# A hybrid decoder layer on one core: the first branch's projection in seven products of quarters, the scores by head pairs

## The chip, the cores and the metric

One core of one Trainium2 chip runs the whole layer. The metric is the device time of one execution in microseconds; the time before is the median of three runs.

## The reference

The layer takes `x` of 256 tokens by 2048 channels. One input projection feeds two token mixers and two gates; each mixer's output is widened by a gate, projected to 2048 channels, merged, projected once more, normed and added to `x`. Everything is float32. Cut to what matters:

```python
h = rms_norm(x, pre_norm_w)
proj = h @ w_in                          # 2048 x 12304
gdn_qkv, gdn_z, gdn_b, gdn_a, moba_qkv, moba_z, gate_a, gate_b = split(proj)
qkv = silu(causal_depthwise_conv(gdn_qkv, conv_w))        # 4 taps
qa, ka, va = ...                         # 8 heads of 128, q and k l2-normed
beta, g = sigmoid(gdn_b), -exp(a_log) * softplus(gdn_a + dt_bias)
oa = gated_delta_rule(qa, ka, va, beta, g)   # chunks of 64: a triangular inverse each
oa = rms_norm_per_head(oa) * gdn_norm_w * silu(gdn_z)
u_a = oa @ w_branch_a                    # 1024 x 2048
ob = causal_softmax_attention(qb, kb, vb)    # 8 heads of 128; one block of 256 here
ob = ob * silu(moba_z)
u_b = ob @ w_branch_b                    # 1024 x 2048
merged = sigmoid(gate_a) * u_a + sigmoid(gate_b) * u_b
y = merged @ w_out                       # 2048 x 2048
out = x + rms_norm(y, post_norm_w)
```

## The kernel before

Tokens lie in two tiles of 128 (`t`), channels in 16 row blocks of 128. A float32 product is made of three reduced-precision ones: each operand is split into `hi` (ScalarE, a cast) and `lo` (VectorE, value minus `hi`), and TensorE adds hi·hi, hi·lo and lo·hi. Weights come through SyncE's queue in pieces of 1 MB (`raw`, three buffers) and are split by `split` (L211) in halves of 128x1024 elements, with three buffers for `hi` and three for `lo`.

Two forms of projection are used. `proj_n` (L347) gives tokens by 512 channels: 12 matmuls of 128x512 for each half. `proj_t` (L329) gives two heads transposed: 8 pairs of a 128x512 and a 128x256 matmul for each half. A `product` (L986) is one quarter (512x512) of the output projection, 12 matmuls for each token tile.

The order of the projections is written out by hand in `ORDER`: names are queries and keys of the first mixer (`q`, `kq`), its values (`v`), its gate (`zg`), the second mixer's values, gate and heads (`mv`, `zm`, `mk`; `mk` makes an `mq` and an `mk` projection for two heads) and the two merge gates (`ga`, `gb`, four column blocks each). The smaller work is written as generators in `Queue`s. After every 6 matmuls of `proj_n` and `product`, and every 8 of `proj_t`, `tick` (L132) counts each queue's wait down by 0.5; when it is up, the next step is issued there, in the midst of a projection. The values yielded are those waits: `SC_WAIT` before a head's scores, `LC_WAIT`, `INV` and `L_WAIT` round the triangular inverse, `SV_WAIT` and `OS_WAIT` in the solve, `A_WAIT1` to `4` in attention.

- `scores` (L491), one head at a time: a split of key and query (`kq`), scores, decays.
- `inverse` (L598): the chunks go to DRAM and back regrouped (`l_d`, `lc`), VectorE makes the inverse in 63 steps (`tv`, `tw`), which goes to DRAM and back (`t_d`, `tt`) by the GpSimd queue.
- `solve` (L695): small matmuls (`sv`, `so`), the norm and gate (`oz`), then `turned_outputs` (L773) transposes by token tile and splits into `oaT`.
- `attend` (L812): scores `ms`, softmax `s`, transposes `pp`, values `po`, the gated output `om`, and its transpose `pt` into `obT`.
- After all gates, a loop over the four column blocks makes `ua` (48 matmuls), multiplies it into `ga`, makes `ub` (48 matmuls), multiplies it into `gb`, and queues `merge` (L925): the sum, transposes `mt`, the split into `mT`, and sums of quarters (`sums`, `sf`).
- The output projection does the upper half of its rows for the first two column blocks in seven quarter products (`yp1` to `yp7`) instead of eight, by sums of quarters of `mT` and differences of quarters of the weights (`tq`, fetched by the GpSimd queue). Third-block pieces `third` (`y2`) lie between. Four PSUM banks (c11, c12, c21, c22) gather the results; `s1`, `s5` and `v` keep copies.

```python
def differences():                       # L917
    yield 3
    for o, a, b in ((0, 0, 2), (1, 1, 0), (2, 1, 2)):
        for u in range(2):
            us = slice(2 * u, 2 * u + 2)
            nc.vector.tensor_tensor(tq[o][:, us], tq[a][:, us], tq[b][:, us], op=ALU.subtract)
            yield 1
```

Each engine runs its instructions in the order in which they were issued; a tile shares its place with another of the same tag, and waits until that one's readers are done.

Of the kernel before, what the change touches and what calls it, by code (L numbers as in the profile page):

```python
# [15 lines left out]
P = 128  # L16
# [10 lines left out]
L_WAIT = 7  # L27
LC_WAIT = (2, 2, 2, 4)
INV = (0.6, 2)
SLOW = 8  # L30
V_WAIT = 8
SV_WAIT = 1
OS_WAIT = 5
# [39 lines left out]
def hybrid_layer(  # L73
# [52 lines left out]
    aq = [Queue(), Queue()]  # L126
# [4 lines left out]

    def tick():  # L132
        after[0] -= 0.5
        for q in (gq, vq, mq, *aq, *extra):
            q.tick()
# [177 lines left out]
    for t in range(NT):  # L313
        dg = wk.tile([P, P], F32, tag="f256", bufs=6, name=f"dg_{t}")
        nc.vector.tensor_scalar_mul(dg, ident, rstd[:, t : t + 1])
        mm(prr[:, t * P : (t + 1) * P], ones, dg, start=True, stop=True)
# [131 lines left out]
    def halves(pt, name):  # L448
        y = wk.tile([P, S], F32, tag="f256", bufs=6, name=f"y_{name}")
# [41 lines left out]
    def scores(h, kT, qT):  # L491
        kq = big.tile([P, 2, 2 * S], F32R, tag=("tt", "tw")[h % 2], name=f"kq_{h}")
        for i, y in enumerate((kT, qT)):
            nc.scalar.copy(kq[:, i, :S], y)
            nc.vector.tensor_tensor(kq[:, i, S:], y, kq[:, i, :S].bitcast(F32), op=ALU.subtract)
        yield SC_WAIT
        p1 = aux_tile(f"s1_{h}")
# [83 lines left out]
    def queries(p):  # L581
        h = 2 * p
        pq = proj_t(CQ + h * P, f"q{h}")
        qTs = [halves(pq[m], f"q{h + m}") for m in range(2)]
        for m in range(2):
            conv_silu(qTs[m], h + m)
        for m in range(2):
            gq.add(scores(h + m, kTs[p][m], qTs[m]))
        if p == H // 2 - 1:
            gq.add(inverse())  # L590
            gq.add(solve())
# [86 lines left out]
    ga = big.tile([P, D // 512, NT, 512], F32, tag="ga", name="ga")  # L678
# [6 lines left out]
    ob_tile = lazily(lambda: free_tile([P, H, 2 * S], F32R, "g0", "obT"))  # L685

    def sigmoid_gate(n, col, c):
        pts = proj_n(w_in, col + c * 512, hT, KT, f"{n}{c}")
        for t in range(NT):
            tl = ga if n == "ga" else gb_tile()  # L690
            nc.scalar.activation(tl[:, c, t, :], pts[t], AF.Sigmoid, scale=rstd[:, t : t + 1])

    oaT = [None]

    def solve():  # L695
# [77 lines left out]
        def turned_outputs(t, oz):  # L773
            for g in range(2):
                pt = aux_tile(f"ot_{t}_{g}")
                for hh in range(4):
                    tr(pt[:, hh * P : (hh + 1) * P], oz[:, g, hh, :], ident)
                p3 = pt.rearrange("p (h n) -> p h n", n=P)
                hi = oT[:, g * 4 : g * 4 + 4, t * P : (t + 1) * P]
                lo = oT[:, g * 4 : g * 4 + 4, S + t * P : S + (t + 1) * P]  # L780
                gn = pcol[:, NTAP * NCV : NTAP * NCV + 1]
                nc.scalar.activation(hi, p3, AF.Copy, scale=gn)
                nc.vector.scalar_tensor_tensor(
                    lo, p3, gn, hi.bitcast(F32), op0=ALU.mult, op1=ALU.subtract
                )
                yield 0.5

# [10 lines left out]
        for t in range(NT):  # L798
            yield from normed(t, ozs[t])
        yield OS_WAIT  # L800
        for t in range(NT):
            yield from turned_outputs(t, ozs[t])
# [9 lines left out]
    def attend(h, qT, kT):  # L812
# [26 lines left out]
        om = wk.tile([P, NT, P], F32, tag="om", name=f"om_{h}")  # L839
        for t in range(NT):  # L840
            nc.vector.scalar_tensor_tensor(
                om[:, t, :], po[:, t * P : (t + 1) * P], sm[:, t : t + 1], zm()[:, t, hc], op0=ALU.mult, op1=ALU.mult
            )
        yield A_WAIT4
        pt = aux_tile(f"pt_{h}")
        for t in range(NT):
            tr(pt[:, t * P : (t + 1) * P], om[:, t, :], ident)
        obT = ob_tile()
        nc.scalar.copy(obT[:, h, :S], pt[:, :S])
        nc.vector.tensor_tensor(obT[:, h, S:], pt[:, :S], obT[:, h, :S].bitcast(F32), op=ALU.subtract)  # L850

    def attention(p):
# [7 lines left out]
        for m in range(2):  # L860
            aq[m].add(attend(h + m, qTs[m], kTs[m]))

# [7 lines left out]
    for blk in ORDER:  # L870
# [11 lines left out]
        elif n == "mk":  # L882
            attention(c)
        else:
            sigmoid_gate(n, {"ga": CGA, "gb": CGB}[n], c)


    gq.drain()
    for q in aq:
        q.drain()  # L890
    mT = big.tile([P, KT, 2 * S], F32R, tag="hT", name="mT")

# [10 lines left out]
    sf = big.tile([P, 4, 4, P], F32, tag="z0", name="sums_f")  # L903


    tq = [None, None, None]

    def load_quarter(i, h, c):
        tq[i] = big.tile([P, 4, 512], F32, tag=f"z{i}", name=f"tq_{i}")
        nc.gpsimd.dma_start(  # L910
            tq[i], wo[h * 512 : (h + 1) * 512, c * 512 : (c + 1) * 512].rearrange("(k p) c -> p k c", p=P)
        )

    load_quarter(1, 1, 1)
    load_quarter(2, 0, 0)

    def differences():  # L917
        yield 3
        for o, a, b in ((0, 0, 2), (1, 1, 0), (2, 1, 2)):
            for u in range(2):  # L920
                us = slice(2 * u, 2 * u + 2)
                nc.vector.tensor_tensor(tq[o][:, us], tq[a][:, us], tq[b][:, us], op=ALU.subtract)
                yield 1

    def merge(c, wait=1):  # L925
        yield wait
        for t in range(NT):
            nc.vector.tensor_tensor(ga[:, c, t, :], ga[:, c, t, :], gb_tile()[:, c, t, :], op=ALU.add)
        yield 0.5
        p3s = []  # L930
        for t in range(NT):
            pt = aux_tile(f"mt_{c}_{t}")
            for q in range(4):
                tr(pt[:, q * P : (q + 1) * P], ga[:, c, t, q * P : (q + 1) * P], ident)
# [9 lines left out]
        if c == 1:  # L944
# [9 lines left out]
            load_quarter(0, 0, 1)  # L954
            formed.append(True)
            sq.add(differences())

    formed = []
    sq = Queue()
    extra.append(sq)  # L960

    for c in range(D // 512):
        pa = proj_n(wa, c * 512, oaT[0], H, f"ua{c}")
        for t in range(NT):
            nc.vector.tensor_tensor(ga[:, c, t, :], ga[:, c, t, :], pa[t], op=ALU.mult)
        pb = proj_n(wb, c * 512, ob_tile(), H, f"ub{c}")
        for t in range(NT):
            nc.vector.tensor_tensor(gb_tile()[:, c, t, :], gb_tile()[:, c, t, :], pb[t], op=ALU.mult)
# [3 lines left out]
    sq.drain()  # L972
    while not formed:
        mq.tick()

    def quarter(t, h):

        ks = slice(4 * h, 4 * h + 4)
        return mT[:, ks, t * P : (t + 1) * P], mT[:, ks, S + t * P : S + (t + 1) * P]

    def load(h, c):
        raw = wraw.tile([P, 4, 512], F32, tag="raw", name=f"raw_y{c}_{h}")
        nc.sync.dma_start(raw, wo[h * 512 : (h + 1) * 512, c * 512 : (c + 1) * 512].rearrange("(k p) c -> p k c", p=P))
        return raw

    def product(a, raw, banks, first, name):  # L986

        for u in range(2):
            hi, lo = split(raw[:, 2 * u : 2 * u + 2, :], [P, 2, 512], f"{name}_{u}")
            for kk in range(2):  # L990
                k = 2 * u + kk
                for (ah, al), pt, new in zip(a, banks, first):
# [133 lines left out]
```

## Time and profile before

| | |
|---|---|
| runs, us | 781.89, 779.69, 779.84 (median 779.84) |
| the profiled execution, us | 780.75 |
| its span, us | 778.8 |
| mean granted TensorE clock | 0.996 |
| TensorE busy | 768.0 us, 99% of the span |
| VectorE busy | 530.7 us, 68% |
| ScalarE busy | 412.1 us, 53% |
| GpSimd busy | 24.6 us, 3% |
| read from and written to HBM | 145.42 and 3.15 MB |

PE is TensorE, DVE VectorE, ACT ScalarE, POOL GpSimd, SP SyncE. In the timeline a line has the start, the duration, the engine, the line of the code, the operation, output and inputs, their shapes, the number of instructions drawn together, and in brackets the idle time before with what ended it. In the groups the numbers after the count are busy time and mean ns of one, then idle time before. In the slices: busy time and count of PE, weight loads, DVE, ACT and POOL, the granted clock, the DMA share and GB/s. A DMA line ends with the KB of one and the median us from issue to landing.

### The profile page before, as it was taken

To read this page: it belongs to the slowest core of one execution; us is meant where nothing else is said; L and a number is where in the kernel's file an instruction comes from. 1 tells how busy PE (TensorE), PEld (TensorE's weight loads), DVE (VectorE), ACT (ScalarE), POOL (GpSimd) and SP (SyncE) were. 2 spreads that over 40 slices of the span, in tenths; PEclk is the share of its full clock that TensorE was granted. 3 is DMA by queue.
4 is the path that set the end of the run, shared out by engine and by line. 5 is a ranking of instruction groups with operands and counts; after the bars stand their busy time and mean duration, and the time that the engine had idled before them with its cause. 6 is when DMAs were issued, how large, how long until landed. Compare 5 with 4: busy or idle time off the path is not lost.

```text
span 778.8 us, 10308 instructions
## 1 busy us (share of the span) xinstructions
PE 768.0 (99%) x3947; PEld 655.4 (84%) x3947; DVE 530.7 (68%) x876; ACT 412.1 (53%) x623; POOL 24.6 (3%) x47
## 2 busy tenths in 40 slices
PE   8999999999999999999999999999999999999996
PEld 7898988898888888888888888888888888888884
DVE  5787668887864898976444665555644668986673
ACT  5677665655565545455435647354454445465451
POOL 3000000010020000001100000000000000000000
PEclk9999999999999999999999999999999999999999
DMA  8576675467479555656943455555456555577442
GB/s 304 169 226 221 185 217 163 134 196 210 162 214 280 180 203 178 201 187 205 230 135 109 152 174 168 187 162 186 162 185 228 183 197 203 192 271 270 166 158 109
DMA packets 92823, 149.24 MB, mean 192 GB/s; under 512 B 3045, under 2 KB 46694, under 8 KB 92134
## 3 DMA queue, kind: packets, MB, share of 16 engines
q1 hardware_dynamic: 89958, 136.51, 54.4%
q0 software_dynamic: 2240, 11.02, 4.8%
q10 hardware_dynamic: 576, 1.05, 0.4%
q8 instruction: 31, 0.51, 0.3%
q14 instruction: 18, 0.15, 0.1%
HBM read 145.42 MB, written 3.15 MB: 191 GB/s over the span
## 4 chain that ended last, share of the span: by engine, by line
PE 95%; DVE 2%; ACT 2%; DMA 1%; issue 0%; SPq 0%; DVEq 0%
PE a_gb L140 11%; PE a_ga L140 11%; PE a_y L140 11%; PE a_k L140 6%; PE a_zg L140 6%; PE a_mq L140 6%; PE a_mk L140 6%; PE a_v L140 6%; PE a_zm L140 6%; PE a_mv L140 5%; PE a_ub L140 5%; PE a_ua L140 5%; PE a_q L140 4%; PE sv L140 2%; PE s L140 1%; PE po L140 1%
## 5 line engine op out<-in xcount | busy, mean ns | idle before, releaser
L140 PE MATMUL a_gb<-hi_gb,hT 128*128 128x512 f32 x256 | 83.2, 396 | 0.0
L140 PE MATMUL a_ga<-hi_ga,hT 128*128 128x512 f32 x256 | 80.7, 391 | 0.0
L215 DVE TENSOR_TENSOR lo_gb<-raw_gb,hi_gb 128x1024 fp32r<-128x1024 f32 x32 | 39.2, 1224 | 41.3 <-ACT hi_gb L214 41.3
L214 ACT CAST hi_gb<-raw_gb 128x1024 fp32r<-128x1024 f32 x32 | 33.7, 1052 | 49.2 <-PE a_gb L140 33.6
L140 PEld LDWEIGHTS a_ga<-hi_ga,hT 128*128 128x128 f32 x256 | 48.1, 188 | 9.9
L140 PEld LDWEIGHTS a_gb<-hi_gb,hT 128*128 128x128 f32 x256 | 48.1, 188 | 9.9
L214 ACT CAST hi_ga<-raw_ga 128x1024 fp32r<-128x1024 f32 x32 | 33.6, 1051 | 37.9 <-PE a_ga L140 28.0
L215 DVE TENSOR_TENSOR lo_ga<-raw_ga,hi_ga 128x1024 fp32r<-128x1024 f32 x32 | 39.1, 1223 | 16.6 <-ACT hi_ga L214 16.3
L140 PE MATMUL a_ga<-lo_ga,hT 128*128 128x512 f32 x128 | 49.9, 390 | 0.0
L140 PE MATMUL a_gb<-lo_gb,hT 128*128 128x512 f32 x128 | 49.8, 389 | 0.0
L140 PE MATMUL a_zg<-hi_zg,hT 128*128 128x348 f32 (+1 forms) x192 | 46.6, 322 | 0.0
L140 PE MATMUL a_mq<-hT,hi_mq 128*128 128x512 f32 x128 | 46.4, 405 | 0.0
L140 PE MATMUL a_mk<-hT,hi_mk 128*128 128x512 f32 x128 | 46.3, 403 | 0.0
L140 PE MATMUL a_y<-hi_y,mT 128*128 128x512 f32 x144 | 45.6, 390 | 0.0
L140 PE MATMUL a_v<-hT,hi_v 128*128 128x512 f32 x128 | 45.6, 399 | 0.0
L140 PE MATMUL a_q<-hT,hi_q 128*128 128x512 f32 x128 | 45.3, 395 | 0.0
L140 PE MATMUL a_ua<-hi_ua,oaT 128*128 128x512 f32 x128 | 41.8, 395 | 0.0
L140 PE MATMUL a_k<-hT,hi_k 128*128 128x512 f32 x128 | 41.1, 404 | 0.2 <-ACT hi_k L267 0.2
L140 PE MATMUL a_zm<-hi_zm,hT 128*128 128x512 f32 x128 | 40.6, 392 | 0.0
L140 PE MATMUL a_mv<-hi_mv,hT 128*128 128x512 f32 x128 | 40.1, 391 | 0.0
L140 PE MATMUL a_ub<-hi_ub,obT 128*128 128x512 f32 x128 | 40.0, 389 | 0.0
L140 PE MATMUL a_v<-hT,lo_v 128*128 128x256 f32 x128 | 35.9, 281 | 0.0
(318 smaller groups left out, 1905.0 us busy)
## 6 DMA issues: line engine op xcount, KB each, us to landing
raw_ga<-in_w_in_dram SPq DMA_DIRECT2D x16, 1024.0 KB, 5.0
raw_gb<-in_w_in_dram SPq DMA_DIRECT2D x16, 1024.0 KB, 5.1
raw_y<-in_w_out_dram SPq DMA_DIRECT2D x15, 1024.0 KB, 5.0
raw_q<-in_w_in_dram SPq DMA_DIRECT2D x8, 1024.0 KB, 5.6
raw_mv<-in_w_in_dram SPq DMA_DIRECT2D x8, 1024.0 KB, 5.1
raw_v<-in_w_in_dram SPq DMA_DIRECT2D x8, 1024.0 KB, 5.7
raw_zm<-in_w_in_dram SPq DMA_DIRECT2D x8, 1024.0 KB, 8.3
raw_mq<-in_w_in_dram SPq DMA_DIRECT2D x8, 1024.0 KB, 5.8
```

The lines of the kernel that those rows point to most:

```text
L140: return pin(nc.tensor.matmul(*args, **kwargs))
L214: nc.scalar.copy(hi, raw)
L215: nc.vector.tensor_tensor(lo, raw, hi.bitcast(F32), op=ALU.subtract)
```

## The change

- *First branch.* `ua` is made by pairs of column blocks (`branch_pair`): seven products of quarters instead of eight for each pair (`seven`, which the output projection uses too). Its weights come as seven quarters through `product`; three of the quarters are fetched by the GpSimd queue and turned into differences ahead (`fetch`, `differences`, `next_differences`), and four sums of quarters of the solve's outputs are formed and split (`oas`). Pieces of the gates ga2 and ga3 (`gate`) lie between the products. The last loop has `ub` alone; the sum ga + gb stands right behind it.
- *Order.* ga1 comes after mk2; `ua0` and `ua1` stand round gb0 and gb1.
- *Scores by head pairs.* Both heads are split, then one `SC_WAIT`, then both heads' scores. `L_WAIT` is 5, `LC_WAIT` (1.5, 1.5, 1.5, 3.5), `OS_WAIT` 3, and the solve's outputs are transposed tile 1 first, eight transposes at a time.
- *Attention outputs.* The gated output is written in its gate's place (`zm`), its transposes are queued apart (`bq`) and held while the sums are formed.
- *Output projection.* c11 is copied from c21 instead of added late; its pieces come as y2, p1, y2, p5, p6, y2, p2, p7, p3, p4.

```diff
-L_WAIT = 7
-LC_WAIT = (2, 2, 2, 4)
+L_WAIT = 5
+LC_WAIT = (1.5, 1.5, 1.5, 3.5)
+T_WAIT = 3
-OS_WAIT = 5
+OS_WAIT = 3
-    "q0 mv0 zg0 q1 kq2 kq3 zg1 v0 v1 v2 ga0 zm0 zm1 ga1 mv1 v3 ga2 ga3 mk0 mk1 gb0 mk2 gb1 mk3 gb2 gb3"
+    "q0 mv0 zg0 q1 kq2 kq3 zg1 v0 v1 v2 ga0 zm0 zm1 mv1 v3 mk0 mk1 mk2 ga1 mk3 ua0 gb0 gb1 ua1 gb2 gb3"
...
-        for q in (gq, vq, mq, *aq, *extra):
+        for q in (gq, vq, mq, *(() if held else aq + bq), *extra):
...
+    def score_pair(h, kT, qT):
+        kqs = []
+        for m in range(2):
+            kq = big.tile([P, 2, 2 * S], F32R, tag=("tt", "tw")[m], name=f"kq_{h + m}")
...
         yield SC_WAIT
+        for m in range(2):
+            yield from scores(h + m, kqs[m], qT[m])
...
+    def fetch(tq, w, c, i):
+        rs, cs = (0, 512, 0)[i], (c + (1, 1, 0)[i]) * 512
+        nc.gpsimd.dma_start(tq[i], w[rs : rs + 512, cs : cs + 512].rearrange("(k p) c -> p k c", p=P))
+
+    def differences(tq, c, wait):
+        yield wait
+        for o, a, b in ((0, 0, 2), (1, 1, 0), (2, 1, 2)):
...
+    def seven(quarter, s_, tq, w, c, banks, name, fill=lambda i: None, done=lambda b: None):
+        c11, c12, c21, c22 = banks
+        s5 = tq[0][:, 0]
+        product([quarter(0, 0)], load(w, 0, c, name), [c21], [True], f"{name}p1")
+        fill(0)
+        product([s_[0]], tq[0], [c12], [True], f"{name}p5")
+        nc.scalar.copy(c11, c21)
+        product([s_[1]], tq[1], [c21], [False], f"{name}p6")
+        nc.scalar.copy(s5, c12)
+        fill(1)
+        raw21 = load(w, 1, c, name)
+        nc.vector.tensor_tensor(c12, c21, s5, op=ALU.add)
+        product([quarter(0, 1)], raw21, [c11], [False], f"{name}p2")
+        for u in range(2):
+            us = slice(2 * u, 2 * u + 2)
+            nc.vector.tensor_tensor(tq[1][:, us], raw21[:, us], tq[1][:, us], op=ALU.subtract)
+        product([s_[2]], tq[2], [c21], [False], f"{name}p7")
+        fill(2)
+        nc.vector.tensor_tensor(c22, c21, s5, op=ALU.add)
+        done(c11)
+        product([s_[3]], load(w, 1, c + 1, name), [c12], [False], f"{name}p3")
+        fill(3)
+        done(c12)
+        done(c22)
+        product([quarter(1, 1)], tq[1], [c21], [False], f"{name}p4")
+        done(c21)
...
+        seven(quarters(oaT[0]), oas, tqs[-1], wa, c, (c11, c12, c21, c22), f"ua{c}", fill=gate, done=done)
...
+        for i in (0, 2, 1):
+            fetch(tqs[0], wa, 0, i)
+        sq.add(differences(tqs[0], 0, T_WAIT))
         yield OS_WAIT
-        for t in range(NT):
-            yield from turned_outputs(t, ozs[t])
+        held.append(True)
+        yield from turned_outputs(ozs)
+        held.pop()
...
-        om = wk.tile([P, NT, P], F32, tag="om", name=f"om_{h}")
+            om = zm()[:, t, hc]
+            nc.vector.scalar_tensor_tensor(om, po[:, t * P : (t + 1) * P], sm[:, t : t + 1], om, op0=ALU.mult, op1=ALU.mult)
+        bq[h % 2].add(turned_attention(h))
...
+    def branch(c):
+        pb = proj_n(wb, c * 512, ob_tile(), H, f"ub{c}")
+        for t in range(NT):
+            nc.vector.tensor_tensor(gb_tile()[:, c, t, :], gb_tile()[:, c, t, :], pb[t], op=ALU.mult)
+        for t in range(NT):
+            nc.vector.tensor_tensor(ga(c, t), ga(c, t), gb_tile()[:, c, t, :], op=ALU.add)
...
-        pa = proj_n(wa, c * 512, oaT[0], H, f"ua{c}")
-        for t in range(NT):
-            nc.vector.tensor_tensor(ga[:, c, t, :], ga[:, c, t, :], pa[t], op=ALU.mult)
...
+        if n == "ua":
+            next_differences(*((wa, 2), (wo, 0))[c])
```

The sums of quarters of the outputs are formed at the end of `turned_outputs`:

```diff
+            oa_f = big.tile([P, 2, 4, P], F32, tag="tv", name="oa_f")
+            x, y = (oa_f[:, i] for i in range(2))
+            nc.scalar.copy(x, a[1, 1])
+            nc.vector.tensor_tensor(a[1, 1], a[1, 0], x, op=ALU.add)
+            nc.scalar.copy(y, a[0, 0])
+            nc.vector.tensor_tensor(a[0, 0], a[1, 1], y, op=ALU.subtract)
+            nc.scalar.copy(x, a[0, 0])
+            yield 0.5
+            nc.vector.tensor_tensor(a[0, 1], a[0, 1], x, op=ALU.subtract)
+            nc.vector.tensor_tensor(a[1, 0], y, a[1, 0], op=ALU.subtract)
...
+                halved(*sums[i], a[o])
```

More of the change, by code (lines that the diff above doesn't have):

```diff
@@ L586, in queries @@
             conv_silu(qTs[m], h + m)
-        for m in range(2):
-            gq.add(scores(h + m, kTs[p][m], qTs[m]))
+        gq.add(score_pair(h, kTs[p], qTs))
         if p == H // 2 - 1:
@@ L695, in solve, with next_differences @@
+    def next_differences(w, c):
+        for q in aq + bq:
+            q.drain()
+        tqs.append([big.tile([P, 4, 512], F32, tag=f"z{i}", name=f"tq{len(tqs)}_{i}") for i in range(3)])
+        for i in (0, 2, 1):
+            fetch(tqs[-1], w, c, i)
+        formed.clear()
+        sq.add(differences(tqs[-1], c, T_WAIT))
     def solve():
@@ L771, in normed @@
                 yield 0.5
[L773 to L785, printed above, removed]
+        gn = pcol[:, NTAP * NCV : NTAP * NCV + 1]
@@ L786, in turned_outputs @@
                 yield 0.5
+            oas.extend(sums)
         while vq.items or v_left[0]:
@@ L972, in hybrid_layer @@
[L972 to L992, printed above, removed]
-                    mm(pt, ah[:, k], hi[:, kk, :], start=(new and k == 0), stop=False, skip_group_check=True)
-                    mm(pt, ah[:, k], lo[:, kk, :], start=False, stop=False, skip_group_check=True)
-                    mm(pt, al[:, k], hi[:, kk, :], start=False, stop=(k == 3), skip_group_check=True)
-                tick()
```

193 lines of the change are left out of this document (118 added, 75 removed).

## The prediction

> **What bounds the kernel now.** I read the busy times and the chain that ended last on the page first, then what TensorE (PE) waited for, then how far apart its matmuls start, then the slices of time in which another engine is nearly full.
>
> ```profile
> span 778.8 us, 10308 instructions
> PE 768.0 (99%) x3947; PEld 655.4 (84%) x3947; DVE 530.7 (68%) x876; ACT 412.1 (53%) x623; POOL 24.6 (3%) x47
> PE 95%; DVE 2%; ACT 2%; DMA 1%; issue 0%; SPq 0%; DVEq 0%
> PE hTp L143 <- DMA x<-in_x_dram: 1.7, 2, 1.1
> PE warm L140 <- DVE epst L174: 1.1, 1, 1.1
> PE a_k L140 <- ACT hi_k L267: 0.2, 1, 0.2
> ```
>
> PE is busy 99% of the span, and all its recorded waits (the last three lines: total, times, longest) are in the first projection. So a matmul taken out shortens the kernel one for one, as long as the operands of the next matmuls are ready that much sooner. Every weight block goes by DMA to SBUF, then ScalarE (ACT) rounds it (`hi`), then VectorE (DVE) subtracts (`lo`), then PE uses both.
>
> ```profile
> 599.89 0.39 PE L140 MATMUL a_ua<-lo_ua,oaT 128*128 128x512 f32 x1
> 600.12 0.61 PE L140 MATMUL a_ua<-hi_ua,oaT 128*128 128x512 f32 x2
> 600.57 0.39 PE L140 MATMUL a_ua<-lo_ua,oaT 128*128 128x512 f32 x1
> 600.79 0.61 PE L140 MATMUL a_ua<-hi_ua,oaT 128*128 128x512 f32 x2
> 601.25 0.39 PE L140 MATMUL a_ua<-lo_ua,oaT 128*128 128x512 f32 x1
> 280.00:300.00 20.00, 20.00 (x90) 16.57 (x89) 19.01 (x35) 9.11 (x10) 0.00 (x0) 1.00 0.55 177
> 660.00:680.00 20.00, 19.89 (x92) 16.03 (x91) 19.34 (x21) 8.02 (x10) 0.00 (x0) 1.00 0.57 199
> 458.12 1.23 DVE L215 TENSOR_TENSOR lo_gb<-raw_gb,hi_gb 128x1024 fp32r<-128x1024 f32 x1 [1.83 <-ACT hi_gb L214]
> 459.26 1.52 DVE L783 SCALAR_TENSOR_TENSOR oaT<-ot,pcol,oaT 128x512 fp32r<-128x512 f32 x2
> ```
>
> A record lasts 0.39 us, but matmuls overlap: six start between 599.89 and 601.25, so one costs 0.227 us. Two units of price follow: a block half (a `hi`/`lo` pair) that feeds 12 matmuls holds PE for 2.73 us, one that feeds 6 for 1.36. One unit of the queues' waits is 12 such matmuls, 2.73 us. DVE records overlap a little too: a `lo` of 1.23 is followed after 1.14. The two slices show DVE at 19.0 and 19.3 of 20 us, and PE loses 0.0 and 0.1: a nearly full DVE does no harm by itself; a queue of DVE work in front of one particular `lo` may.
>
> **Part 1: the products (-5.45).** A column block of the first branch has 8 row blocks x 2 token tiles x 3 = 48 matmuls, a pair of blocks 96, that is 8 quarter products of 12. The change does 7 of 8 in each of two pairs: 2 x 12 = 24 matmuls fewer, and none elsewhere. 24 x 0.227 = 5.45 us, all on PE's path.
>
> **Part 2: the narrow place at the projection mq6 (+2.3; 0.9 to 7).** The fetch of the first pair's three quarters is issued when the solve's outputs are normed; the differences follow T_WAIT = 3 units later, 8.2 us. In DVE's new order two of them (`tq_g`) stand straight ahead of the `lo` of the first half of mq6, so that `lo` and all of DVE wait for 2 MB of DMA. Between that `lo` and the next one, mq6_0_1, stand the softmax of two heads, four more differences and four `oaT` halves, which in the kernel before lie apart, between gate blocks.
>
> ```profile
> 473.69 0.35 DVE L820 SCALAR_TENSOR_TENSOR s<-ms,qscale,mask_m 128x128 f32<-128x128 f32 x1 [1.09 <-PE ms L140]
> 476.25 0.17 DVE L826 RECIPROCAL sm<-sm 128x2 f32<-128x2 f32 x1
> L922 DVE TENSOR_TENSOR tq<-tq,tq 128x1024 f32<-128x1024 f32 x6 | 7.2, 1218 | 0.0
> L783 DVE SCALAR_TENSOR_TENSOR oaT<-ot,pcol,oaT 128x512 fp32r<-128x512 f32 x4 | 3.0, 748 | 0.0
> 468.26 0.60 PE L143 MATMUL pt<-ident,om 128*128 128x128 f32 x4
> 468.62 0.48 PE L140 MATMUL a_gb<-hi_gb,hT 128*128 128x512 f32 x1
> 472.84 1.47 PE L140 MATMUL ms<-y_mk,y_mq 128*128 128x128 f32 x8
> 473.96 0.58 PE L140 MATMUL a_mq<-hT,hi_mq 128*128 128x512 f32 x1
> 480.03 0.28 PE L140 MATMUL a_mq<-hT,lo_mq 128*128 128x256 f32 x1
> 478.07 2.36 DVE L215 TENSOR_TENSOR lo_mq<-raw_mq,hi_mq 128x1024 fp32r<-128x1024 f32 x2 [0.77 <-ACT hi_mq L214]
> 471.36 1.28 ACT L691 ACT_TABLE_LOAD   x1
> 472.66 1.26 ACT L691 ACTIVATE gb<-a_gb,rstd 128x512 f32<-128x512 f32 x2
> 473.94 1.28 ACT L824 ACT_TABLE_LOAD   x1
> 477.01 1.98 ACT L214 CAST hi_mq<-raw_mq 128x1024 fp32r<-128x1024 f32 x2
> ```
>
> The place is tight already: from 471.36 to 477.01 ACT is held by two table loads, a gate and the softmax, and the third `lo` of an mq block is done at 478.07 + 1.22 = 479.3, when PE asks for it at 480.03. Only 0.7 us was left. After the change DVE has, from the first head's scores on: softmax 2.4 (473.69 to 476.25, less a gap), four differences 4 x 1.14 = 4.6, four `oaT` 4 x 0.67 = 2.7, reciprocals 0.1, and the `lo` 1.2: 11.0, and 0.1 for the hand-over, 11.1 us. PE needs in the same stretch 18 gate matmuls (4.1), eight pairs of mq6 (2.8: from 473.96 to 480.03 lie two such sets, a break and the first matmul of a third), 16 transposes (1.4: four in 0.36, 468.26 to 468.62) and the second head's scores (0.6: two heads in 1.12, 472.84 to 473.96): 8.9. DVE is 2.2 us late; ACT, with two table loads, exps, gates and four `oaT` in the same stretch, by my sum of its rows only 0.9, so DVE sets the price.
>
> ```profile
> tq<-in_w_out_dram POOLq DMA_DIRECT2D x3, 1024.0 KB, 6.5
> hx<-in_x_dram POOLq DMA_DIRECT2D x1, 2048.0 KB, 8.3
> ```
>
> Ahead of all this comes the fetch: 2 MB took 8.3 us in the nearest row (`hx`), against 8.2 of waiting: 0.1 more, 2.3 in all. The bounds: 0.9 if DVE catches up by its lead, 7 if the two megabytes come one after the other, as two `tq` rows would (13.0, so 4.8 late). The Trainium skill ("DMA: Bandwidth & Descriptors", section "Anatomy of one DMA") fits a GpSimd-issued transfer by 2.0 us plus its bytes at 436 GB/s, an estimated 6.8 us for 2 MB, by which the fetch never waits and the sum would be 0.1 less; the 6.5 and 8.3 us of these rows, with weights loading beside them, are slower than that fit.
>
> **Part 3: the products of the pairs (+0.5; 0 to 1.5).** A single product asks a `lo` of 1.14 and a `hi` of ACT every 1.36 us of PE, double the rate of before; a gate piece is put between most of them, in which the same costs are spread over 2.73. Seven products and four gate pieces take PE 7 x 2.73 + 4 x 5.45 = 40.9 us. DVE does 22 `lo` (25.1), two differences (2.3), two sums of banks and four gate products (6 x 0.6 = 3.6): 31 of 41 us, less dense than the two slices above, so only single late `lo`s, after attention work, are priced. The copies between the banks and the casts of ACT (53% busy) lie under a product of 2.73 us at least.
>
> **Part 4: the second branch alone (+0.9; 0 to 3).** Before, the merge lay beside `ua` and `ub`; now only `ub` (4 x 48 x 0.227 = 43.6 us) and the transposes (some 3) are left there.
>
> ```profile
> L940 DVE TENSOR_TENSOR mT<-mt,mT 128x512 fp32r<-128x512 f32 x8 | 5.4, 687 | 0.0
> L928 DVE TENSOR_TENSOR ga<-ga,gb 128x512 f32<-128x512 f32 x8 | 5.2, 684 | 0.0
> ```
>
> DVE has 16 `lo` (18.3), three times eight operations of 0.6 (14.4: gate by branch, the addition, `mT`), eight for the quarter sums (4.8) and six differences (6.9), 44 us of 47: as dense as 660 to 680, but for the whole stage. I take 0.9: two transposes that wait for the addition, which now comes right behind `ub`, and a late `lo` or two; less the 0.1 that 660 to 680 lost before.
>
> **Part 5: the output (+0.4; 0 to 1.8).** Products p2, p7, p3 and p4 now follow each other: PE 10.9 us, DVE 8 `lo` (9.1), two differences (2.3), two bank sums (1.2), 12.6. The 1.7 lacking are mostly in hand in the three split buffers.
>
> **Part 6: scores, inverse, sums (0).** Scores by pairs move work of both kinds unchanged; the solve starts some 24 us earlier and the inverse with it, but L_WAIT falls from 7 to 5, so the way from the inverse to its use is 5.5 us shorter. The rows:
>
> ```profile
> 366.22 2.58 POOL L640 DMA_DIRECT2D t_d<-tv  x4 [137.66 <-DVE tv L637]
> 372.44 2.73 POOL L646 DMA_DIRECT2D tt<-t_d  x4 [3.64 <-issue]
> tt<-t_d POOLq DMA_DIRECT2D x4, 128.0 KB, 5.3
> 389.40 1.85 PE L140 MATMUL sv<-gdn,tt 64*64 64x128 f32 x15
> ```
>
> The last `tt` landed near 372.4 + 2.7 + 5.3 = 380.4, the first product with it is at 389.4: 9.0 spare, 3.5 after the change. It still hides. The quarter sums, `oa_f` and the outputs written over the gate are 0.6 each on ACT and DVE, and counted in their queues above or hidden there.
>
> **The sum.** The profiled execution took 780.75 us (span 778.8 and 1.95 around it), 0.91 over the median of the runs, 779.84. -5.45 + 2.3 + 0.5 + 0.9 + 0.4 - 0.1 = -1.45: 779.3 against that execution, 778.4 against the median. 0.3%, or 2.3 us, is about what a measurement of this kernel can tell from no change.
>
> **The rivals.** *The cover holds.* PE records no wait in 700 us, and DVE at 97% cost 0.1: if the lead of the split buffers takes up parts 2 to 5 but for two microseconds at most, 774.4 to 776.4. Against it stands the 0.7 us that is left at mq today.
>
> *The fetch is late: slower.* One mechanism, at `tq_g` ahead of mq6: if it lands 13.0 us after its issue, DVE's queue and then PE stop for 7.0 instead of 2.3, +3.25: 783.1. It decides from a landing 12.1 us after issue, where part 2 reaches 6.1 and the sum is 2.3 slower. For it: three transfers at once beside the weights, 3 MB where `hx` is 2. So long a stop can cost more:
>
> ```profile
> 5.00:10.00 5.00, 3.75 (x18) 3.02 (x18) 2.64 (x6) 2.90 (x6) 3.34 (x3) 0.75 1.00 343
> 10.00:15.00 5.00, 5.00 (x32) 4.51 (x31) 2.83 (x6) 2.35 (x6) 0.00 (x0) 0.91 1.04 388
> ```
>
> The granted clock (third from the end) was 0.75 and 0.91 after the thin start, worth 5 x 0.25 + 5 x 0.09 = 1.7 us; the same again after a stop gives 784.8. The Trainium skill ("TensorE: Matmul & The Clock Gate", Part 1) says the clock falls to half after an idle window of about 3.4 us and needs as long busy to return; the start agrees, but no later row shows a stop.
>
> *The inverse is late.* If the 3.5 us of part 6 are overrun by 4, as one `t_d` landing late behind weights would, +2.5: 782.4. That the change does not do what it says is no rival: the 24 matmuls are gone from PE's order.
>
> **How the numbers follow.** My forecast 0.48 (its own range 776.6 to 780.6; 0.14 of it faster, 0.34 the same), the cover 0.24 (faster), the late fetch 0.17 (slower), the late inverse 0.11 (0.02 the same, 0.09 slower). So 0.38 faster, 0.36 the same, 0.26 slower. The range 774.8 to 783.0 leaves out about half of the cover's best and half of the late fetch, some 0.2.
>
> **What would show it.** Right: PE busy about 5.5 us less; waits of PE on `lo_mq`, 2 us or so at one place, from DVE; single waits in the second branch; none on `tt`. Wrong: a wait of DVE on the DMA of `tq_g` of several microseconds, a granted clock under 1 after it, waits on `tt`, or no waits at all. The forecast falls if the waits sum to under 2 or over 7 us.

## The result and the profile after

| | before | after |
|---|---|---|
| runs, us (median) | 779.69 to 781.89 (779.93) | 790.05, 790.07, 791.56, 791.79 (790.82) |
| ratio, 95% interval | | 1.0135 [1.0113, 1.0157] |
| profiled execution and its span, us | 780.75, 778.8 | 790.07, 788.4 |
| mean granted clock | 0.996 | 0.994 |

The kernel became 10.9 us slower. The forecast was 778.4 in a range up to 783.0: its sign and its range are wrong. These are the page's busy times after:

```profile
span 788.4 us, 10325 instructions
PE 767.4 (97%) x3923; PEld 651.6 (83%) x3923; DVE 565.0 (72%) x914; ACT 425.3 (54%) x642; POOL 29.0 (4%) x53
```

The 24 matmuls are gone (3947 to 3923), but PE, busy for almost as long as before, now stands still for 21.0 us of the span instead of 10.8 (a stalled or slowed matmul counts as busy for longer). PE's waits, which were all in the first projection before, are now in the middle as well. The seven largest behind the first projection (total, times, longest):

```profile
PE a_mq L144 <- ACT hi_mq L218: 2.8, 1, 2.8
PE a_ga L144 <- DVE lo_ga L219: 2.2, 3, 1.1
PE a_gb L144 <- DVE lo_gb L219: 1.7, 1, 1.7
PE a_mq L144 <- DVE lo_mq L219: 1.1, 1, 1.1
PE a_v L144 <- DVE lo_v L219: 0.8, 1, 0.8
PE a_ub L144 <- DVE lo_ub L219: 0.5, 1, 0.5
PE a_y L144 <- DVE lo_y L219: 0.4, 1, 0.4
```

I price a stop by the distance of two matmul starts, less the 0.227 (512 columns) or 0.117 (256) that it takes undisturbed. The largest is at mq6. The timeline of PE there:

```profile
438.10 0.28 PE L144 MATMUL a_mq<-hT,lo_mq 128*128 128x256 f32 x1
441.19 0.80 PE L144 MATMUL a_mq<-hT,hi_mq 128*128 128x512 f32 x1 [2.81 <-ACT hi_mq L218]
443.11 0.58 PE L144 MATMUL a_mq<-hT,lo_mq 128*128 128x256 f32 x1 [1.12 <-DVE lo_mq L219]
443.49 0.63 PE L144 MATMUL a_mq<-hT,hi_mq 128*128 128x512 f32 x1
444.13 0.63 PE L144 MATMUL a_mq<-hT,hi_mq 128*128 128x512 f32 x1
...
447.97 0.40 PE L144 MATMUL a_mq<-hT,hi_mq 128*128 128x512 f32 x1
```

Three starts in a row come 2.98, 1.69 and 0.27 late: 4.9 us. Then a pair takes 0.64 (443.49 to 444.13) instead of 0.35, seven times, until 447.97: 2.0 more. The slices show why (PEclk third from the end):

```profile
440.00:441.10 1.10, 0.00 (x0) 0.00 (x0) 1.10 (x2) 1.10 (x3) 0.00 (x0) 1.00 0.00 0
441.20:447.90 6.70, 5.58 (x16) 4.39 (x17) 6.70 (x11) 4.55 (x7) 0.00 (x0) 0.50 0.52 156
448.00:454.00 6.00, 6.00 (x35) 5.11 (x35) 4.25 (x6) 3.91 (x6) 0.00 (x0) 1.00 0.51 175
```

The granted clock fell to 0.50 between 441.1 and 441.2, right ahead of the first late start and so before the 1.69, and was back 6.8 us later. The Trainium skill ("TensorE: Matmul & The Clock Gate", Part 1) says that the clock halves after an idle window of about 3.4 us and returns after as long a busy one. The trace agrees that a stop halves it and that it returns while PE works; but here the clock fell when PE had stood still for 2.9 us (438.2 to 441.1), and the measurement decides. The last section says more.

What VectorE did ahead of it, the fetch it waited for, and two rows of ScalarE:

```profile
417.51 1.53 POOL L724 DMA_DIRECT2D tq_g<-in_w_branch_a_dram  x2 [55.36 <-ACT jo L882]
428.79 2.36 DVE L731 TENSOR_TENSOR tq_g<-tq_g 128x1024 f32<-128x1024 f32 x2 [2.94 <-DMA tq_g<-in_w_branch_a_dram]
431.07 1.22 DVE L219 TENSOR_TENSOR lo_mq<-raw_mq,hi_mq 128x1024 fp32r<-128x1024 f32 x1
432.20 0.35 DVE L987 SCALAR_TENSOR_TENSOR s<-ms,qscale,mask_m 128x128 f32<-128x128 f32 x1
...
438.26 2.35 DVE L731 TENSOR_TENSOR tq_g<-tq_z,tq_g 128x1024 f32<-128x1024 f32 x2
440.52 1.40 DVE L911 SCALAR_TENSOR_TENSOR oaT<-ot,pcol,oaT 128x512 fp32r<-128x512 f32 x2
441.84 1.21 DVE L219 TENSOR_TENSOR lo_mq<-raw_mq,hi_mq 128x1024 fp32r<-128x1024 f32 x1
...
433.17 0.40 ACT L991 ACTIVATE s<-s,mx 128x128 f32<-128x128 f32 x1 [3.79 <-DVE mx L989]
440.08 1.06 ACT L218 CAST hi_mq<-raw_mq 128x1024 fp32r<-128x1024 f32 x1
```

The difference could start 11.3 us after the fetch was issued. VectorE has no gap from 428.79 until 449, and 10.8 us lie between the two `lo_mq`. PE's first wait there ends with ScalarE's `hi_mq`, not with a `lo`: ScalarE had waited 3.79 us for VectorE's row maxima and then had its softmax, `oaT` halves, a table load and ga1's gates ahead of `hi_mq`, almost without a gap. The `lo` that ends the stop began 0.7 us after that `hi_mq` was done, behind VectorE's own queue, so VectorE sets the 4.9 as a whole.

The other stops, by the same measure: gb0 1.85 at 513.7; ga3 0.53 at 573.2 and 1.31 at 595.7; the stage of `ub` 0.29 + 0.33 (two transposes `mt`) + 0.64 (`lo_ub`); v 1.03 at 203.1; ga2 0.81 at 485.7; `y` 0.53. With mq6's 6.9 these are 14.2 us; less 5.45 for the matmuls, 8.8 of the 9.6 by which the spans differ. The order at gb0 and at the second stop of ga3:

```profile
513.91 0.69 DVE L804 TENSOR_TENSOR ga<-ga,a_ua 128x512 f32<-128x512 f32 x1 [3.15 <-PE a_ua L144]
514.51 3.49 DVE L219 TENSOR_TENSOR lo_gb<-raw_gb,hi_gb 128x1024 fp32r<-128x1024 f32 x3
594.84 1.23 DVE L731 TENSOR_TENSOR tq<-tq,tq 128x1024 f32<-128x1024 f32 x1 [2.04 <-DMA tq<-in_w_out_dram]
595.99 1.22 DVE L219 TENSOR_TENSOR lo_ga<-raw_ga,hi_ga 128x1024 fp32r<-128x1024 f32 x1
```

At gb0 the multiplication of the gate by the last product must wait for that product's last matmul, and the `lo` that PE needs next stands behind it. At ga3 a difference waits for its fetch, and again a `lo` stands behind. At v, ScalarE waits for the weights:

```profile
202.03 1.05 ACT L218 CAST hi_v<-raw_v 128x1024 fp32r<-128x1024 f32 x1 [5.60 <-DMA raw_v<-in_w_in_dram]
200.00:204.00 4.00, 3.57 (x19) 2.61 (x17) 0.89 (x1) 1.97 (x3) 0.00 (x0) 1.00 1.08 358
```

The DMA share (second from the end) is over 1 there: the solve's chunks (`lc`, 2 MB), issued at 184.6 instead of 226.6 before because of the pairs of scores, are loaded beside v's weights instead of beside zm's.

### The profile page after: what moved, and what is told of

It is laid out like the page before. It is cut to its first block, busy times and chain, and to the rows that moved or that the text cites. A ratio compares the mean times of both kernels' runs of the same rounds, so it can differ in the third digit from the quotient of the medians.

```text
span 788.4 us, 10325 instructions
## 1 busy us (share of the span) xinstructions
PE 767.4 (97%) x3923; PEld 651.6 (83%) x3923; DVE 565.0 (72%) x914; ACT 425.3 (54%) x642; POOL 29.0 (4%) x53
## 5 line engine op out<-in xcount | busy, mean ns | idle before, releaser
L144 PE MATMUL a_ga<-hi_ga,hT 128*128 128x512 f32 x256 | 84.1, 396 | 0.0
L144 PE MATMUL a_gb<-hi_gb,hT 128*128 128x512 f32 x256 | 79.2, 389 | 0.0
L144 PE MATMUL a_mq<-hT,hi_mq 128*128 128x512 f32 x128 | 48.7, 419 | 2.8 <-ACT hi_mq L218 2.8
L144 PE MATMUL a_mq<-hT,lo_mq 128*128 128x256 f32 x128 | 37.1, 290 | 1.1 <-DVE lo_mq L219 1.1
```

Of the source, the lines that this page charges most:

```text
L144: return pin(nc.tensor.matmul(*args, **kwargs))
```

## The experiments

Two theories stood at first. *Fetch*: mq6 loses its time because `tq_g` lands late. *Queue*: too much VectorE work stands beside mq6 and mk6 whatever the fetch does. The order of the instructions on VectorE showed a thing that the text ahead of the prediction has wrong: a step's wait does not settle the place of its instructions, since an instruction may be put ahead of others that were issued before it. `pin` keeps it where its step is issued. In the changed kernel VectorE is ready for the first difference 8.3 us after the fetch was issued, ahead of `lo_mq`; with the same 3 units and `pin` it starts 15.0 us after it (433.67, the fetch at 418.69), behind `lo_mq` and the scores of two heads. A hold below means a wait with `pin`. Each ratio is against the runs of the kernel before on the same chip (medians 780.2 to 780.9, against 779.93 above), so two versions that lie within about 1 us are not told apart.

**What 24 matmuls are worth.** The kernel before, with the 12 matmuls of one token tile on the lower half of the rows left out in `ua1` and in `ua3` (`u_a` then lacks them):

```diff
-                    for t in range(NT):
+                    for t in range(1 if less and kb == 1 else NT):
```

> The kernel before, with one quarter product of eight left out in each pair of column blocks of ua (24 matmuls of 128x512, so u_a lacks them); everything else as before. If TensorE's own work sets the time, as the prediction has it, this is 24 x 0.227 = 5.45 us faster, 774.4, with no new wait. If something else sets the pace in that stretch (casts, lo, weights), the gain is clearly less than 5 us and a wait of PE on lo_ua or lo_ub takes its place.

Measured 778.96, ratio 0.9981 [0.9970, 0.9992]: -1.8 us, not -5.45. Waits of PE came up that the kernel before does not have, and the slice at 660 shows them with VectorE at 18.97 of 20 us. (The profiled execution, 781.33, was one of the two slowest of ten; the other eight lie at 779.8 or below. 3.4 us at half clock are in its slice, and the others may not have them.)

```profile
PE a_ub L140 <- DVE lo_ub L215: 1.8, 1, 1.8
PE a_ua L140 <- DVE lo_ua L215: 1.1, 1, 1.1
660.00:680.00 20.00, 17.09 (x71) 13.32 (x70) 18.97 (x21) 7.37 (x8) 0.00 (x0) 0.91 0.56 197
```

Where VectorE is nearly full, as in this stretch of the kernel before, only a third of PE's saved time was time saved.

**The first differences held back, 3 units and 6 units.** Two runs:

```diff
-        sq.add(differences(tqs[0], 0, T_WAIT))
+        sq.add(differences(tqs[0], 0, 3, pin))      # second run: 6
```

> The changed kernel with the first pair's six differences held in program order on VectorE: the two of tq_g now come behind lo_mq6_0_0 and the two heads' scores, three of six still ahead of lo_mq6_0_1, the rest between the next lo. Theory A (the fetch lands 2.9 us later than VectorE reaches tq_g, and the stop of PE at mq6 with the half clock after it is its result): the DMA wait is gone, PE stops for 2 us or less at mq6, the granted clock stays at 1.00, and the kernel is 4 to 6 us faster than the changed one, 785 to 787. Theory B (the queue of some 11 us of VectorE and ScalarE work at mq6 is enough by itself): the stop stays over 3 us, the clock falls again, gain under 2 us, 789 to 791.

> As the run before, but the first differences start 6 units after the norms instead of 3, so that all six come behind lo_mq6_0_1, one between each of the next lo. Both theories expect no stop at the first halves of mq6 and no fall of the clock: 783 to 785, some 7 us faster than the changed kernel. If the time is that of the run before, the queue costs nothing once the fetch is out of the way; if it is 2 us or more better, the queue has its own price. A stop at mk6 or at the first product of ua0 instead would show that the work was only moved.

Measured 790.67 (1.0130 [1.0114, 1.0145]) and 790.16 (1.0121 [1.0106, 1.0136]). VectorE's wait on the fetch is gone, the clock stays at 1.00, and no more than 0.7 us came back: the stops are 0.68, 1.98, 1.74 and 0.67 at mq6 with 1.0 at mk6 in the first run, 0.68, 1.03, 1.74, 0.67 and 1.0 in the second. *Fetch* fell as the cause: the first run's expectation for it, 785 to 787, is missed, and so is the second run's 783 to 785. One stop became several, as *queue* has it. But the queue is not VectorE's alone. In the second run VectorE itself waits for ScalarE ahead of `lo_mq`:

```profile
434.63 1.41 DVE L911 SCALAR_TENSOR_TENSOR oaT<-ot,pcol,oaT 128x512 fp32r<-128x512 f32 x2 [1.06 <-ACT oaT L910]
438.37 1.41 DVE L911 SCALAR_TENSOR_TENSOR oaT<-ot,pcol,oaT 128x512 fp32r<-128x512 f32 x2 [2.33 <-ACT oaT L910]
439.87 1.23 DVE L219 TENSOR_TENSOR lo_mq<-raw_mq,hi_mq 128x1024 fp32r<-128x1024 f32 x1
```

The first two stops (0.68 and 1.03) stand behind ScalarE's `hi_mq`, which ends at 439.8 behind `oaT`, a table load and ga1's gates; the later ones behind VectorE's sums and differences.

**The last gate multiplication behind the next `lo`.**

```diff
-        done(c21)
+        if name != "y":
+            lq.add(later(done, c21))     # 0.5 units later, held there
```

> The changed kernel, but the last gate multiply of a pair (the one that waits for the last matmul of p4) is held on VectorE behind the first lo of the next gate block instead of ahead of it. If that in-order wait makes PE wait 1.7 us for lo_gb at 513.7 us, the wait falls to 0.3 or less and the kernel is 1.2 to 2 us faster, 789. If lo_gb is late for another reason (ScalarE's table load and gate evictions ahead of hi_gb), there is no gain.

Measured 789.87 (1.0116 [1.0091, 1.0142]). The stop at gb0 went from 1.85 to 0.39, nearly the 0.3 that was expected; the time fell by 1.0, less than its interval of 2 us either way can tell. In its profiled run v lost more than in the changed kernel (1.00 and 1.03, with half clock behind), which hides part.

**The outputs later; then outputs and differences apart; then all of it.** `OS_WAIT` 6 alone; with the first differences held for 6 units; and with the later multiplication and the other differences held for 4 too:

```diff
-OS_WAIT = 3
+OS_WAIT = 6
-        sq.add(differences(tqs[0], 0, T_WAIT))
+        sq.add(differences(tqs[0], 0, 6, pin))      # second and third run
-        sq.add(differences(tqs[-1], c, T_WAIT))
+        sq.add(differences(tqs[-1], c, 4, pin))     # third run
```

> The changed kernel with OS_WAIT 6 instead of 3: the solve's outputs are transposed, split and summed beside mk6 instead of mq6; the fetch and its differences stay ahead of lo_mq6_0_0, in the order of the changed kernel. If the late fetch alone makes the stop, it stays at 2.5 us or more with a fall of the clock, and the gain is under 2.5 us (788 or more). If the outputs' queue (four oaT halves on both engines ahead of the second half of mq6) is what the delay adds up with, the stop is under 2.5 us, the clock stays at 1.00 and the gain is 4 to 6 us, 785.

> OS_WAIT 6 and the first differences held in program order 6 units after the norms, so that neither stands between the first halves of mq6. If the place is a sum of the two, PE stops for 1 us or less in all from mq6 to mk6, at a clock of 1.00, and the kernel is 6 to 8 us faster than the changed one: 782.5 to 784.5. If the work was only moved, stops of 3 us or more appear at mk6 or ua0.

> As the run before, with the last gate multiply of each pair behind the next gate block's first lo, and the differences of the second and third fetch held in program order 4 units after their fetch. Expected: the waits at gb0 (1.7) and at the last piece of ga3 (1.1) fall to 0.5 together, so 2 us better than the run before: 780.5 to 782.5, about the kernel before. What then remains over 5.45 us less than before is single waits at v, ga2, ub and y. If other waits grow by as much as these fall, the time is that of the run before.

Measured 788.73 (1.0101 [1.0084, 1.0119]), 789.65 (1.0120 [1.0103, 1.0137]) and 787.38 (1.0086 [1.0071, 1.0102]). In the first VectorE still waits 2.83 us for the fetch; the stop at mq6 is 1.93 and 1.36, but the clock stays at 1.00, which neither case of its expectation has. In the last two almost nothing is left at mq6, and the stop went to mk6 in one piece: 3.58, the case "only moved" of the second run's expectation. The third run is 2.3 faster than the second, as expected of the two holds at gb0 and ga3 (0.42 and no stop left there), but from 789.65. Its longest wait, VectorE's rows ahead of it and two slices:

```profile
PE a_mk L144 <- DVE lo_mk L219: 3.4, 1, 3.4
447.67 1.22 DVE L219 TENSOR_TENSOR lo_mk<-raw_mk,hi_mk 128x1024 fp32r<-128x1024 f32 x1
...
457.56 1.21 DVE L219 TENSOR_TENSOR lo_mk<-raw_mk,hi_mk 128x1024 fp32r<-128x1024 f32 x1
455.00:460.00 5.00, 1.59 (x7) 1.18 (x6) 5.00 (x7) 2.41 (x4) 0.00 (x0) 0.89 0.01 3
460.00:465.00 5.00, 5.00 (x24) 4.29 (x23) 4.28 (x5) 1.32 (x2) 0.00 (x0) 0.77 0.27 75
```

Between two `lo` lie 9.9 us of differences, `oaT` halves, sums and their splits without a gap. ScalarE is in time here: its `hi_mk` for the second of these was done at 450.7. The work was moved along, not made to fit.

**The scores by pairs alone**, put into the kernel before (`score_pair` as in the change's diff, its waits left).

> The kernel before with the scores by head pairs alone. The last scores come some 30 us earlier, so the 2 MB of lc are fetched beside the v projections, whose weights come in 1 KB rows, instead of beside zm. If that contention is the wait of 0.8 us at v in the changed kernel, PE waits there for 0.5 to 1.5 us on hi_v or lo_v, and the time is 0 to 2 us over the kernel before. If the wait there has to do with the other changes, nothing is slower, and the time is that of before within 0.3%.

Measured 782.65 (1.0027 [1.0018, 1.0036]): 2.1 us. PE's new waits are 0.8 on `lo_v` and 0.2 on `hi_v`, and ScalarE waits 5.7 us for `raw_v` as in the changed kernel. So this part is priced, and it is the change's own.

**ga1 between mk3 and ua0**, with the holds: `OS_WAIT` 6.5, the first differences held for 4.5 units, the others for 4, the multiplication later.

```diff
-... mk0 mk1 mk2 ga1 mk3 ua0 gb0 gb1 ua1 gb2 gb3
+... mk0 mk1 mk2 mk3 ga1 ua0 gb0 gb1 ua1 gb2 gb3
```

> The edits of all apart, with the gate ga1 and the projection block mk3 in the other order, so that the first differences, the outputs' halves and the sums lie beside a gate block (12 matmuls, 2.73 us of PE for each lo) instead of two projections of heads, OS_WAIT 6.5 and the differences 4.5 units after the norms: one or two operations stand between two lo. The theory of the full VectorE (some 22 us of differences, halves and sums are more than the stretch beside mq6 and mk6 has room for, wherever they are put in it) expects the stop of 3.4 us at mk6 and the fall of the clock to vanish, stops under 1 us in the whole stretch, and 6 us less than all apart: 781 to 783. The rival, that the stop is made by the order of a few instructions, expects it to appear again at ga1, and 786 to 788.

Measured 781.5, 1.0011 [1.0000, 1.0022]: 9 of the 11 us are back. VectorE is as full as ever there, but PE loses only 0.6 us in one place and no clock. A gate block asks for a `lo` every 2.73 us, and mostly one or two other operations stand between two of them:

```profile
440.00:460.00 20.00, 19.54 (x97) 16.03 (x96) 19.16 (x24) 13.70 (x20) 0.00 (x0) 1.00 0.44 154
```

Its profiled execution was the slowest of its ten (784.24), with a stop of 1.32 + 1.03 at v and 3.4 us at half clock behind it.

**The same, with ga0 ahead of v** (`zg1 ga0 v0 v1 v2 zm0`, `OS_WAIT` 6, first differences 4), to take v away from `lc`.

> As the run before, and the gate block ga0 ahead of the values v0 to v2 in the order, so that lc lands beside a gate block with 2 KB rows instead of beside the values. If the contention of lc with 1 KB rows is the wait at v (0.8 to 1.3 us of PE, and 2 us of time in the run with score pairs alone), it vanishes: 1 to 2 us less than the run before, 779.5 to 781.5, about the kernel before. If lc delays whatever is beside it, the wait moves to ga0 and the time stays.

Measured 785.23 (1.0053 [1.0032, 1.0075]): a miss. v keeps its waits (0.8 and 0.8), and new ones of 1.1 on `hi_ga` and 0.4 on `lo_ua0p` came. It did not take v away from `lc`: v's first weights are fetched some 15 us ahead of their use, so `lc` (issued at 186.1) still lies beside two `raw_v` (187.4 and 192.2), and the run does not tell whether v's 1 KB rows matter.

**The scores one head at a time again**, in the version with ga1 moved; the second run also with the old waits around the inverse.

```diff
-        gq.add(score_pair(h, kTs[p], qTs))
+        for m in range(2):
+            gq.add(scores(h + m, kTs[p][m], qTs[m]))
-LC_WAIT = (1.5, 1.5, 1.5, 3.5)      # second run
+LC_WAIT = (2, 2, 2, 4)
-L_WAIT = 5
+L_WAIT = 7
```

> The kernel of the run with ga1 between mk3 and ua0 (781.5, 1.0011 of the kernel before), with the scores one head at a time again, as before. Theory (the pairs of scores put the regrouping loads lc of the chunks beside the fetch of the v weights): the two stops at a_v near 204 us, 1.3 and 1.0 there, go to under 0.4 in all, and the time falls by the 2.1 that the pairs cost alone, to 779.4 (778.4 to 780.5), ratio 0.998. Rival (the solve and its outputs come some 24 us later and fall on the projections of the attention heads or on gb0 instead): a_v is rid of its stops, but new stops of 1 us or more stand on lo_mk, lo_gb or at ua0, and the time is 781.5 or more. Rival (the stop at a_v belongs to the order around v and not to the scores): a_v keeps its stops, 781.5.

> As the run beside it, and the waits round the inverse are those of the kernel before too (LC_WAIT 2, 2, 2, 4 and L_WAIT 7). Theory: as beside it, 779.4 (778.4 to 780.5): no stop at a_v. Rival (outputs of the solve too late): with 5.5 us and more of further waiting the outputs reach ua0 late or fall on gb0, stops there of 1 us or more, 781.5 or more; the difference between the two runs is then the price of the waits.

Measured 794.29 (1.0177 [1.0161, 1.0193]) and 797.37 (1.0214 [1.0191, 1.0237]): a clear miss, and the first rival's case; the old waits cost 3.1 more. v is rid of its stops, but zm has them now (2.1 and 0.8 of waits), and the solve's outputs come too late for ua0. (The kernel before loads `lc` beside zm too and has no stop there; why is open.) The first run's waits:

```profile
PE ms L144 <- DVE oas L913: 4.9, 1, 4.9
PE a_zm L144 <- ACT hi_zm L218: 2.1, 1, 2.1
PE a_ua L144 <- DVE oaT L913: 1.4, 1, 1.4
```

The pairs of scores cost 2 us at v, and are worth 12.8 (794.3 to 781.5) to a kernel that wants the outputs at ua0, with the other waits left as they are.

**ga1 moved alone**, without any hold.

> The changed kernel (790.8) with one edit: ga1 stands between mk3 and ua0 instead of between mk2 and mk3. Theory (VectorE has too much work beside mq6 and mk6: outputs, sums, differences and softmax; where a gate block comes behind mk3, the same work has 22 us more before ua0 asks for it): most of the loss goes by the order alone, the stop at mq6 and the half clock behind it (7.1) fall to 3 or less, and the time is 783 to 787. Rival (the holds on the differences and on the outputs did it): with the differences still ahead of the halves of the weights, the stop at mq6 stays as it is, and the time is 789 to 791. Rival (the fetch of tq_g landing late is the cause): as the rival before, with VectorE's wait on that transfer of 2 us or more.

Measured 789.58 (1.0109 [1.0095, 1.0124]): the theory missed its 783 to 787. The fetch is waited for again (1.96), and the stop at mq6 became four on the halves of ga1, of 1.39, 1.39, 1.64 and 0.73:

```profile
PE a_ga L144 <- DVE lo_ga L219: 7.1, 7, 1.5
440.00:460.00 20.00, 15.48 (x67) 11.50 (x66) 17.30 (x21) 10.29 (x15) 0.00 (x0) 1.00 0.47 158
```

The time is that of the rivals, 789 to 791. So neither does it alone: the order returns 1.2, the holds 3.4 (787.38), both 9.3. (The holds' waits differ a little, `OS_WAIT` 6 and 6 units there against 6.5 and 4.5; that difference was not run by itself.)

**`lc` by SyncE's queue**, in between v's weights, in the version with ga1 moved.

```diff
-            nc.gpsimd.dma_start(
+            nc.sync.dma_start(
                 lc[32 * g : 32 * g + 32]...
```

> The kernel of e9 (781.5) with one edit: the four loads lc of the regrouped chunks go by SyncE's queue, in between the v weights, instead of by GpSimd's beside them. Theory (the small rows of the v weights starve beside the bulk of lc): in one queue the weights come in turn, raw_v lands no later than one lc load more, the two stops at a_v (1.3 and 1.0) fall to 0.5 or less in all, and the time is 779.0 to 780.5, below the kernel before by 0.1 to 0.2%. Rival (it is the bytes: 2 MB more on the same engines ahead of a buffer that v needs): the stops stay or grow, 781.5 to 784. Rival (SyncE waits for l_d and holds all weights back): a stop of several us near 190 to 205 and 785 or more.

Measured 788.50 (1.0100 [1.0084, 1.0117]): a miss. The DMA lines of this run, then of the version that it changes:

```profile
raw_v<-in_w_in_dram SPq DMA_DIRECT2D x8, 1024.0 KB, 10.6
lc<-l_d SPq DMA_DIRECT2D x4, 512.0 KB, 8.9
```

```profile
raw_v<-in_w_in_dram SPq DMA_DIRECT2D x8, 1024.0 KB, 5.7
lc<-l_d POOLq DMA_DIRECT2D x4, 512.0 KB, 9.1
```

In turn or beside each other, 2 MB more ahead of v's weights are 2 MB more: PE waits 4.9 on `hi_v` instead of 1.2, and the clock falls. The rival that it is the bytes holds in kind, though its 781.5 to 784 is exceeded. The last rival, whose 785 or more fits the time, does not: SyncE issued the next `raw_v` 4.4 us after the one before (181.71 and 186.12), as in the version without this edit (182.76 and 187.13). Of the versions that compute the whole layer none beats the kernel before.

## Why the prediction was wrong

- **Part 1 (-5.45).** The count was right, and the sum below gives the changed kernel its 5.45, since no wait on a `lo_ua` stands in for it. The reason given for "one for one" was not right. It rested on the slice 660 to 680, full VectorE and 0.1 lost, read as "does no harm". The 24-fewer run shows the other half of that reading: with PE in balance with a full VectorE, matmuls taken out there turn into waits (1.8 of 5.45 arrived).
- **Part 2 (+2.3; 0.9 to 7), the largest mis-sized term: 6.9, at the far end of its bounds.** The sum of VectorE's work to the second `lo` was good (11.0 said, 10.8 measured). The landing was not: 8.3 from `hx`, 11.3 measured, so 3.0 more, and with it the stop of 4.9 follows (2.3 + 3.0 = 5.3 by the prediction's arithmetic). The clock added 2.0, which the prediction has in a rival alone. And the working stopped at that `lo`. When the wait on the fetch was removed, 5.1 to 6.1 us were still lost from mq6 to mk6, since ScalarE's gates and halves come first and VectorE's sums, splits and differences go on until 458 in the 6-unit run. The term to work out was VectorE's whole load from the scores to ua0, and ScalarE's beside it, against PE's whole time there.
- **"Three units later."** 8.2 us was about what the changed kernel has (VectorE is ready for the difference 8.3 us after the issue), but `T_WAIT` is not what sets it, as the 15.0 us of the hold show; this is where the order had to be read, not the waits. The number was right by luck.
- **Part 3 (+0.5; 0 to 1.5), the second: 4.5.** No wait on a `lo_ua` appears, so the products' double rate costs nothing, as said. The stops are at the gate pieces between the products and at gb0 behind them: gb0 1.85, ga3 1.31 and 0.53, ga2 0.81. The first two are an instruction that waits for something other than weights, in front of a weight half's `lo`; I had counted those operations by their duration only. The holds took nearly all of both (0.4 is left at gb0). The last two, 1.3 together, are a `lo` behind several other operations, at ga2 the softmax of two heads, which is what the term had priced.
- **Part 4 (+0.9)** measured 1.26, half at two transposes that wait for the addition and half on one `lo_ub`, as it said. **Part 5 (+0.4)** measured 0.53. Both right.
- **Part 6 (0).** No wait on `tt` appears, and so the rival of the late inverse did not come; but this was closer than the 3.5 us said. The solve came 22 us sooner (its first product at 367.4 instead of 389.4), and the last `tt`, issued at 361.5, took 7.1 us where the rows before had 5.3, so that it landed 1.2 us behind the start of that first product. What I did not follow is the other end of the same chain: the earlier scores bring `lc` onto v's weights, 1.0 in the profile after and 2.1 by the pairs-alone run.
- **The rivals.** The late fetch came nearest: the wait of VectorE on `tq_g`, the stop and the clock's fall all appeared. It gave 783.1 or 784.8, though, deciding from a landing at 12.1, and the holds show that its mechanism was not what had to be cured. What I took for bounded single places was, from mq6 to ua0, one budget, overdrawn in one stretch.

The measured terms sum to -5.45 + 6.9 + 4.5 + 1.3 + 0.5 + 1.0 = +8.8, against 9.6 between the spans; the last 0.8 I have not assigned. That the move of ga1 and the holds together do far more than either is shown; which of the held steps matters most in that version is not.

## What to carry to other kernels

An engine that is full beside a busy TensorE is a price waiting to be paid: work out its whole load between two fixed points against TensorE's whole time there, not to the next operand, and do not count a matmul saved there in full until the full engine's work is cut too (here a third of it arrived). In the order of a full engine, look for instructions that wait for something else (a fetch, the last matmul of a product) right in front of an operand that TensorE needs: there the price is the wait, not the duration. And when a chain starts sooner, follow its first transfers as well as its last.

## What the runs showed of the hardware

- The clock changes in steps. Between the first 13 and the last 6 us of all these traces it is at 1.00 or 0.50, and each stretch at 0.50 lasted 3.41 us or two or three times that (6.83 at mq6); the stretches at 1.00 between are whole multiples of 3.41 too. The 0.91, 0.89 and 0.77 of single slices above are means over both. An estimate from these traces: I cut them into these steps and added up, in each step at full clock behind the first 60 us, the time that PE lost by late starts. Steps with up to 1.9 us were followed by full clock (1.85 at gb0, 1.93 with `OS_WAIT` 6 alone), steps with 2.02 and more by half (2.02 at v with ga1 moved, 2.93 at mq6, 3.36 at mk6); two of 1.97 and 1.98 went either way. So some 2 us lost within one step of 3.41 cost clock here, and the same time split by a step's end does not: four stops of 0.73 to 1.64 with some 3 us of matmuls between them left it at 1.00. The idle window of about 3.4 us of the Trainium skill ("TensorE: Matmul & The Clock Gate", Part 1) agrees with the length of a step, but the step need not be idle as a whole.
- A bulk load beside 1 MB weight loads does not stretch all alike: `raw_v` has a median of 5.7 us, but one of the eight, issued 0.2 us behind the last `lc`, took 15.7, with the DMA share at 0.94 to 1.20 until it landed.
- 2 MB fetched by GpSimd beside the weights were usable after 11.3 us. The fit of the Trainium skill ("DMA: Bandwidth & Descriptors", "Anatomy of one DMA") makes that an estimated 6.8, taken as one transfer; here two of 1 MB took it, with a third behind them and weights loading beside them, and the measurement decides.
